# Dilated attention in an encoder trunk: the products of probabilities and values of two heads in one matmul, by halves of the residues

## The chip, the cores and the metric

The kernel runs on one core of a Trainium2 chip. Times are microseconds of device time of that core (us). The core has TensorE (PE: matmuls, with its weight loads, PEld), VectorE (DVE), ScalarE (ACT), GpSimd (POOL) and SyncE (SP, which here issues most of the transfers). Each of them works through its own queue in order and waits for the others by semaphores.

## The reference, cut to what matters

A trunk of two layers is applied to two sequences of 512 tokens. Each layer has four attention branches fed from one input projection; their gated outputs are merged and projected. The change is in the fourth branch, dilated attention: three groups of keys, each seen through its own stride and window, with one softmax over all of them in the end.

```
D_GROUPS = ((128, 1), (512, 4), (2048, 16))
...
o, lse = _banded_attention(to_strided(q), to_strided(k), to_strided(v), window // (2 * dil), D_BLOCK, HEAD_DIM ** -0.5)
...
w = softmax(stack(lses, axis=0), axis=0)
o = einsum('nbthg,nbthgd->bthgd', w, stack(outs, axis=0))
```

The branch has four query heads and two key and value heads, so that two query heads share a key and a value head. That is the pair that the kernel works on.

## The kernel before, in words

A pass is one layer of one sequence; there are four: layer 0 of the first and the second sequence, then layer 1 of both. In a pass everything lies with the channel on the partitions and the 512 tokens along the free axis. Tokens are ordered by their residue modulo 4: four blocks of 128 columns, one for each residue.

Precision comes from splitting. A float32 value is rounded to the matmul's type (hi) and the difference kept (lo), so that a projection takes three matmuls (`mm3`, L153 to L155: hi by hi, hi by lo, lo by hi), and a product with the softmax's probabilities takes two, one with the high part of the probabilities and one with the low part. The weights of the value matrix hold hi in 64 columns and lo in the other 64, so the output has 128 rows, and `finish` (L326) adds the upper 64 to the lower: a copy on ScalarE (L330), a sum on VectorE (L331). `split` (L169) is a cast on ScalarE (L170) and a subtraction on VectorE (L171).

`dilated_pair` (L463) works on one pair of heads. Scores of all groups are computed by matmuls into two PSUM banks named ss (L479, L383, L384), and moved with scale and mask to a score buffer s of 128 x 2048 for each head (L481, L492): columns 0 to 511 for the group of stride 4, 512 to 1023 for stride 16, 1024 to 2047 for the near group in four parts n. Then, head by head: the maximum over the keys (a fold on VectorE, an all-reduce over partitions on GpSimd, L318), its subtraction (L507, L509, L511), the exponentials (L508, L512), and the sums (L499 to L502, later L323). Last, again head by head, the products with the values go into the one PSUM bank named so: for the two strided groups 4 residues x hi and lo, each 128 columns (L522, L523); for the near group 4 parts x hi and lo, each 256 columns (L527, L532). `finish` empties the bank before the next head may use it.

The same bank so and the same two buffers s serve the heads of the other three branches (`dense_head`, L353, and `window_pair`, L403), the loading of the inputs (`load`, `begin`) and so on. Before, s is a tag with two buffers: whoever takes one waits until every reader of the tile that lay there is done.

What stands in which order on each queue is not written by hand. The program is traced step by step (the table `steps`, L800: both pairs of the fourth branch first, D of 1 and D of 0, then the latents LAT, part of the gates G, the latent heads A, and so on), and a scheduler then moves each instruction ahead to where its model of the engines has a free place, by the instruction's place in the trace. So matmuls of later projections fill TensorE while a softmax is under way. Weights come through SP's queue into three buffers wr (L125), are rounded on ScalarE (L131) into wh, and their low parts either computed on VectorE (L110) or, where an earlier pass has stored them, loaded (L134). GpSimd's queue holds the all-reduces alone.

Of the kernel before, what the change touches and what calls it, by code (L numbers as in the profile page):

```python
# [13 lines left out]
P = 128  # L14
T = 512
# [13 lines left out]
def trunk(ctx, tc, x0, x1, wp, wr, wu, wg, wb, wm, wo, vec, rope, msk, eye, y0, y1):  # L29
# [18 lines left out]
    for args in first:  # L48
        new(*args)

# [10 lines left out]
    def pso():  # L61
        return bank("so", 1)
# [4 lines left out]
    def f(ap):  # L67
        return ap.bitcast(F32)
# [257 lines left out]
    def finish(y, rows, o):  # L326

        a, b = rows
        u = new("u", [P, T], F32, 2)
        nc.scalar.copy(out=u[a:b], in_=o[64:128])  # L330
        tt(out=y[a:b], in0=o[0:64], in1=u[a:b], op=ALU.add)  # L331
# [21 lines left out]
    def dense_head(scores, v, scale):  # L353

        s = new("s", [P, 4 * T], F32, 2)
# [47 lines left out]
    def window_pair(q, k, v, z, l, sink):  # L403
        ss = [new("s", [P, 4 * T], F32, 2) for _ in range(2)]
# [58 lines left out]
    def dilated_pair(qs, ks_, vs, z, l):  # L463

        ss = [new("s", [P, 4 * T], F32, 2) for _ in range(2)]
# [28 lines left out]
        for h in range(2):  # L494
# [18 lines left out]
            tots.append(fold(ALU.add))  # L513
        y = new("yf", [P, T], F32, 1)
        for h in range(2):
            s = ss[h]
            o = pso()
            for gi in (1, 2):
                ph, pl = halves(s[:, (gi - 1) * 512 : gi * 512])
                for c in range(4):  # L520
                    sl = slice(c * P, (c + 1) * P)
                    mm(o[:, sl], vs[gi][:, c, :], ph[:, sl], start=gi + c == 1, stop=False, skip_group_check=True)  # L522
                    mm(o[:, sl], vs[gi][:, c, :], pl[:, sl], start=False, stop=False, skip_group_check=True)  # L523
            ph, pl = halves(s[:, 1024:1536])
            for n in (0, 1):
                for x in (ph, pl):
                    mm(span(o, *D_Q[n]), vs[0][:, D_K[n], :], span(x, *D_Q[n]), start=False, stop=False, skip_group_check=True)  # L527
            ph, pl = halves(s[:, 1536:2048])
            for n in (2, 3):
                for x in (ph, pl):  # L530
                    w = by4(x[:, (n - 2) * 256 : (n - 1) * 256])
                    mm(span(o, *D_Q[n]), vs[0][:, D_K[n], :], w, start=False, stop=n == 3 and x is pl, skip_group_check=True)  # L532
            finish(y, (64 * h, 64 * h + 64), o)
            rr.append(total(tots[h]))
# [5 lines left out]
    def load(l, q_, xin, yout):  # L540
        src = xin if l == 0 else saved[q_]
        xt = []
        for h in range(2):
            xl = new("s", [P, 4 * T], F32, 2)
# [23 lines left out]
    def begin(xin):  # L568
# [5 lines left out]
        early = [new("s", [P, 4 * T], F32, 2) for _ in range(2)]  # L574
# [448 lines left out]
```

## Time and profile before

| what | value |
|---|---|
| median of 3 runs | 2161.22 us (2159.58 to 2166.14) |
| the profiled execution | 2158.01 us, its span 2156.2 us |
| instructions | 29144, of them 9550 matmuls |
| granted TensorE clock, mean | 0.989 |
| GpSimd | 419.3 us busy, 19% |
| moved by DMA | 402.29 MB |

The span is the time from the first to the last instruction of the one profiled execution. An engine's busy time is the sum of its instructions' durations without overlap; a matmul's duration holds its way through the array, and matmuls overlap, so that what a matmul costs in a row of them is read from the distance between starts. The chain of waits is followed back from the last instruction: at each step to what released it, or to the instruction before it on its engine. A row of a group of instructions gives line, engine, operation, output and inputs, shape and count, and behind the bar the busy time and the mean in ns, then the idle time before them and who ended it. Lines are those of the kernel before; the lines of the changed kernel are higher by up to 28 behind the products, and by 8 ahead of it.

### The profile page before, as it was taken

How to read it: one execution, taken by the hardware profiler on the slowest of the kernel's cores; microseconds unless marked ns; L12 is line 12 of the kernel's file. 1: busy time of each engine (PE TensorE's matmuls, PEld its weight loads, DVE VectorE, ACT ScalarE, POOL GpSimd, SP SyncE). 2: the span in 40 equal slices, each digit the busy share in tenths (PEclk: the TensorE clock that was granted, in tenths of full speed). 3: DMA queues.
4: the chain of work that ended last, by engine and by line, in shares of the span. 5: the costliest groups of instructions: out<-in, count | busy, mean ns of one | idle time of the engine just before them, and what ended most of it. 6: DMA issues, size and time to landing. Idle time of an engine off the chain costs nothing.

```text
span 2156.2 us, 29144 instructions
## 1 busy us (share of the span) xinstructions
PE 2089.8 (97%) x9550; PEld 1714.5 (80%) x9550; DVE 1795.5 (83%) x3113; ACT 1310.9 (61%) x2229; POOL 419.3 (19%) x145
## 2 busy tenths in 40 slices
PE   7999989999999999999999999999999999999998
PEld 5887778877887787887888877888878887788887
DVE  7999999987489998997537999898866889997725
ACT  6746765544576777755456576754556757685434
POOL 0032213320002230222001322132200232122200
PEclk9999999999999999999999999999999999999999
DMA  6443444556877566678675434545666544455565
GB/s 216 162 148 116 152 140 154 183 186 207 284 247 226 177 227 220 222 243 280 216 232 164 150 120 142 164 155 181 224 203 226 156 152 133 149 161 166 182 215 182
DMA packets 207656, 402.29 MB, mean 187 GB/s; under 512 B 23312, under 2 KB 32016, under 8 KB 206736
## 3 DMA queue, kind: packets, MB, share of 16 engines
q1 hardware_dynamic: 199008, 383.62, 54.7%
q10 hardware_dynamic: 8496, 16.81, 2.3%
q8 instruction: 75, 1.23, 0.2%
q14 instruction: 77, 0.63, 0.1%
HBM read 306.49 MB, written 93.85 MB: 186 GB/s over the span
## 4 chain that ended last, share of the span: by engine, by line
PE 75%; DVE 14%; DMA 4%; ACT 3%; issue 2%; SPq 0%; POOL 0%; DVEq 0%; ACTq 0%; POOLq 0%
PE mm L153 22%; PE mm L154 22%; PE mm L155 22%; DMA wr<-wp 2%; DVE wl L110 2%; DVE ph L171 1%; PE so L375 1%; PE so L374 1%; DMA s<-x 1%; PE ss L383 1%; PE ss L384 1%; ACT wh L131 1%; PE mi L300 1%; ACT rs L242 1%; PE ss L154 1%
## 5 line engine op out<-in xcount | busy, mean ns | idle before, releaser
L153 PE MATMUL mm<-xn,wh 128*128 128x512 f32 x1992 | 782.3, 393 | 3.8 <-ACT wh L131 2.0
L154 PE MATMUL mm<-xn,wh 128*128 128x512 f32 x1992 | 780.1, 392 | 5.1 <-DVE xn L556 5.1
L155 PE MATMUL mm<-xn,wl 128*128 128x512 f32 x1992 | 780.1, 392 | 1.0 <-DMA wl<-lo 1.0
L131 ACT CAST wh<-wr 128x512 fp32r<-128x512 f32 (+1 forms) x596 | 385.7, 651 | 344.5 <-PE mm L154 228.1
L153 PEld LDWEIGHTS mm<-xn,wh 128*128 128x128 f32 x1992 | 374.8, 188 | 83.2 <-ACT wh L131 3.2
L154 PEld LDWEIGHTS mm<-xn,wh 128*128 128x128 f32 x1992 | 375.0, 188 | 81.2 <-DVE xn L556 5.4
L155 PEld LDWEIGHTS mm<-xn,wl 128*128 128x128 f32 x1992 | 374.9, 188 | 80.0 <-DMA wl<-lo 2.3
L323 POOL PARTITION_ALL_REDUCE mr<-mr x64 | 247.9, 3873 | 521.1 <-DVE mr L379 252.6
L318 POOL PARTITION_ALL_REDUCE mr<-mr x64 | 129.2, 2019 | 924.8 <-DVE mr L502 533.0
L110 DVE TENSOR_TENSOR wl<-wr,wh 128x512 fp32r<-128x512 f32 (+2 forms) x304 | 238.6, 786 | 37.5 <-ACT wh L131 20.9
L171 DVE TENSOR_TENSOR ph<-s,ph 128x512 fp32r<-128x512 f32 (+2 forms) x256 | 186.6, 735 | 15.8 <-ACT ph L170 11.9
L170 ACT CAST ph<-s 128x512 fp32r<-128x512 f32 (+2 forms) x256 | 145.0, 577 | 23.3 <-PE so L451 8.2
L242 ACT COPY rs<-mm 32x512 f32<-32x512 f32 x240 | 138.7, 578 | 25.7 <-DVE rx L237 20.3
L153 PE MATMUL mm<-qk,wh 128*128 128x512 f32 (+1 forms) x328 | 124.2, 383 | 8.3 <-ACT wh L131 5.8
L154 PE MATMUL mm<-qk,wh 128*128 128x512 f32 (+1 forms) x328 | 124.8, 382 | 5.8 <-DVE qk L835 5.6
L155 PE MATMUL mm<-qk,wl 128*128 128x512 f32 (+1 forms) x328 | 124.5, 381 | 0.6 <-DVE wl L110 0.3
L153 PE MATMUL mm<-y,wh 128*128 128x512 f32 x256 | 102.8, 405 | 14.0 <-DVE mg L768 11.6
L746 DVE SCALAR_TENSOR_TENSOR th<-th,mm 128x512 f32<-128x512 f32 x96 | 65.2, 681 | 59.0 <-PE mm L155 56.2
L745 ACT ACTIVATE th<-mm 128x512 f32<-128x512 f32 x96 | 57.3, 597 | 81.6 <-PE mm L155 80.9
L155 PE MATMUL mm<-y,wl 128*128 128x512 f32 x256 | 101.2, 395 | 0.0
L154 PE MATMUL mm<-y,wh 128*128 128x512 f32 x256 | 101.1, 395 | 0.0
L359 ACT ACTIVATE s<-ss 128x512 f32<-128x512 f32 x128 | 71.3, 596 | 34.2 <-DVE ph L171 17.3
(183 smaller groups left out, 3292.6 us busy)
## 6 DMA issues: line engine op xcount, KB each, us to landing
wr<-wp SPq DMA_DIRECT2D x310, 256.0 KB, 2.9
wl<-lo SPq DMA_DIRECT2D x250, 256.0 KB, 2.9
wr<-wm SPq DMA_DIRECT2D x192, 320.0 KB, 3.2
lo<-wl SPq DMA_DIRECT2D x200, 256.0 KB, 2.0
lo<-wl SPq DMA_DIRECT2D x96, 320.0 KB, 2.3
wl<-lo SPq DMA_DIRECT2D x96, 320.0 KB, 3.1
wr<-wo SPq DMA_DIRECT2D x68, 256.0 KB, 3.5
wr<-wg SPq DMA_DIRECT2D x64, 256.0 KB, 2.8
```

Of the source, the lines that this page charges most:

```text
L110: tt(out=lo[:, :n], in0=raw[:, :n], in1=f(hi[:, :n]), op=ALU.subtract)
L131: nc.scalar.copy(out=hi[:, :n], in_=raw[:, :n])
L153: mm(ps, wh, xh, start=first, stop=False)
L154: mm(ps, wh, xl, start=False, stop=False)
L155: mm(ps, wl, xh, start=False, stop=last)
L170: ins = nc.scalar.copy(out=hi, in_=src)
L171: tt(out=lo, in0=src, in1=f(hi), op=ALU.subtract)
L242: nc.scalar.copy(out=xs[c : c + 32], in_=ps[o : o + 32])
L318: nc.gpsimd.partition_all_reduce(m, t, P, RED.max)
L323: nc.gpsimd.partition_all_reduce(s, t, P, RED.add)
L359: act(out=s[:, j * T : (j + 1) * T], in_=ps, func=AF.Copy, scale=scale)
L746: stt(out=th, in0=th, scalar=1.0, in1=pb, op0=ALU.add, op1=ALU.mult)
```

## The change

The two score buffers become the two halves of one tile `both_s`, taken in turn by `scores_tile`; `dilated_pair` begins with half 0, so that its two heads lie in one tile at a fixed distance. The products then take columns of both heads at once. The 512 columns of the bank so are 2 heads x 256; the pass over the four residues is cut into two halves of two residues each, and `finish` takes a range of columns. The sums, maxima and exponentials are as they were.

```diff
+    both_s = new("s", [P, 2, 4 * T])
+    turn = [0]
+
+    def scores_tile():
+
+        turn[0] ^= 1
+        return both_s[:, turn[0] ^ 1, :]
...
-    def finish(y, rows, o):
+    def finish(y, rows, o, t=slice(0, T)):
...
-        nc.scalar.copy(out=u[a:b], in_=o[64:128])
-        tt(out=y[a:b], in0=o[0:64], in1=u[a:b], op=ALU.add)
+        nc.scalar.copy(out=u[a:b, t], in_=o[64:128])
+        tt(out=y[a:b, t], in0=o[0:64], in1=u[a:b, t], op=ALU.add)
...
-        ss = [new("s", [P, 4 * T], F32, 2) for _ in range(2)]
+        turn[0] = 0
+        ss = [scores_tile() for _ in range(2)]
...
+        def both(f):
+            hi = new("ph", [P, T], F32R, 6)
+            lo = new("ph", [P, T], F32R, 6)
+            src = f(both_s)
+            hh, ll = (x.rearrange("p (h x) -> p h x", h=2) for x in (hi, lo))
+            if len(src.shape) == 4:
+                hh, ll = (x.rearrange("p h (n x) -> p h n x", n=2) for x in (hh, ll))
+            split(hh, ll, src)
+            return hi, lo
+
+        for half in range(2):
+            o = pso()
+            o4 = o.rearrange("p (h c i) -> p h c i", h=2, c=2)
+            for gi in (1, 2):
+                base = (gi - 1) * 512 + 256 * half
+                pair = both(lambda s: s[:, :, base : base + 256])
+                for c in range(2):
+                    for x in pair:
+                        x4 = x.rearrange("p (h c i) -> p h c i", h=2, c=2)
+                        mm(o4[:, :, c, :], vs[gi][:, 2 * half + c, :], x4[:, :, c, :], start=gi + c == 1 and x is pair[0], stop=False, skip_group_check=True)
+            pair = both(lambda s: s[:, :, 1024 + 256 * half : 1280 + 256 * half])
+            for n in (0, 1):
+                a, b = D_Q[n][0] // 4, D_Q[n][1] // 4
+                for x in pair:
+                    x4 = x.rearrange("p (h c i) -> p h c i", h=2, c=2)
+                    mm(o4[:, :, :, a:b], vs[0][:, D_K[n], :], x4[:, :, :, a:b], start=False, stop=False, skip_group_check=True)
...
+            t = slice(256 * half, 256 * half + 256)
+            for h in range(2):
+                finish(y, (64 * h, 64 * h + 64), o[:, 256 * h : 256 * h + 256], t)
         for h in range(2):
-            s = ss[h]
-            o = pso()
-            for gi in (1, 2):
-                ph, pl = halves(s[:, (gi - 1) * 512 : gi * 512])
-                for c in range(4):
-                    sl = slice(c * P, (c + 1) * P)
-                    mm(o[:, sl], vs[gi][:, c, :], ph[:, sl], start=gi + c == 1, stop=False, skip_group_check=True)
-                    mm(o[:, sl], vs[gi][:, c, :], pl[:, sl], start=False, stop=False, skip_group_check=True)
...
-            finish(y, (64 * h, 64 * h + 64), o)
             rr.append(total(tots[h]))
```

In the changed kernel the products stand in L545 (strided groups), L551 and L557 (near group), `split` in L178 and L179, `finish` in L338 and L339, the eviction of scores in L490 and L501 (L367 in `dense_head`), the exponentials in L517 and L521, a projection's three matmuls in L161 to L163. The scheduler makes of it another order. TensorE before, the first pair of the first pass, first head (`so` is the result's bank, `ph` the split probabilities, `v` the values, `mm` a projection that fills):

```order
L523 MATMUL so_699<-ph_701,v_561 128x128
L522 MATMUL so_699<-ph_700,v_561 128x128
L523 MATMUL so_699<-ph_701,v_561 128x128
L522 MATMUL so_699<-ph_700,v_561 128x128
L523 MATMUL so_699<-ph_701,v_561 128x128
L522 MATMUL so_699<-ph_700,v_561 128x128
L523 MATMUL so_699<-ph_701,v_561 128x128
L522 MATMUL so_699<-ph_712,v_564 128x128
L154 MATMUL mm_1144<-xn_65_217,wh_1167 128x512
L523 MATMUL so_699<-ph_713,v_564 128x128
L522 MATMUL so_699<-ph_712,v_564 128x128
```

The same pair in the changed kernel, both heads, first half of the residues:

```order
L545 MATMUL so_696<-ph_697,v_560 128x2x128
L163 MATMUL mm_1468<-xn_61_204,wl_1472 128x512
L161 MATMUL mm_1468<-xn_62_208,wh_1491 128x512
L162 MATMUL mm_1468<-xn_62_208,wh_1491 128x512
L545 MATMUL so_696<-ph_698,v_560 128x2x128
L545 MATMUL so_696<-ph_697,v_560 128x2x128
L545 MATMUL so_696<-ph_698,v_560 128x2x128
L545 MATMUL so_696<-ph_705,v_563 128x2x128
L163 MATMUL mm_1468<-xn_62_208,wl_1492 128x512
L161 MATMUL mm_1468<-xn_63_212,wh_1491 128x512
L162 MATMUL mm_1468<-xn_63_212,wh_1491 128x512
L545 MATMUL so_696<-ph_706,v_563 128x2x128
```

Eight narrow products of a group become four wide ones for both heads, and the first product of the pair stands at row 423 of TensorE's queue where it stood at row 346: projections went ahead of it. VectorE before, the end of the first pair (`s_613` is the second head's buffer; `s_1189` belongs to the second pair, and takes the first head's buffer):

```order
L171 TENSOR_TENSOR ph_733<-s_612,ph_732 128x512
L247 TENSOR_TENSOR rx_1076<-rx_1076,rs_1077 128x512
L502 TENSOR_TENSOR mr_680<-mr_680,s_613 128x4x64
L481 SCALAR_TENSOR_TENSOR s_1189<-ss_1191,band_340 128x4x64
L481 SCALAR_TENSOR_TENSOR s_1189<-ss_1196,band_340 128x4x64
L110 TENSOR_TENSOR wl_1449<-wr_1446,wh_1448 128x512
L350 SCALAR_TENSOR_TENSOR z_1187<-th_1185,mm_1144 128x512
L272 TENSOR_TENSOR qk_1085<-rx_1076,qk_1085 64x512 x2
L110 TENSOR_TENSOR wl_1497<-wr_1494,wh_1496 128x512
L507 TENSOR_TENSOR s_613<-s_613,mr_685 128x1024
```

The same place in the changed kernel, where all score buffers are the one tile `s_79`:

```order
L179 TENSOR_TENSOR ph_753<-s_79,ph_752 128x512
L339 TENSOR_TENSOR yf_695<-so_696,u_729 64x256
L213 TENSOR_SCALAR ms_1451<-rs_1449 128x16
L118 TENSOR_TENSOR wl_1637<-wr_1634,wh_1636 128x512
L490 SCALAR_TENSOR_TENSOR s_79<-ss_1176,band_339 128x4x64 x2
L490 SCALAR_TENSOR_TENSOR s_79<-ss_1181,band_339 128x4x64 x2
L186 TENSOR_SCALAR nw_1454<-ms_1451 128x16
L339 TENSOR_TENSOR yf_695<-so_696,u_732 64x256
```

Before, the second pair's first scores are evicted (L481) ahead of the second head's exponentials (their subtraction is L507); after, they stand (L490) behind the split of the second half of the residues (`ph_753`), and the bank so is emptied in pieces of 64x256 (L339).

More of the change, by code (lines that the diff above doesn't have):

```diff
@@ L353, in dense_head @@
     def dense_head(scores, v, scale):
-        s = new("s", [P, 4 * T], F32, 2)
+        s = scores_tile()
         for j in range(4):
@@ L463, in dilated_pair @@
     def dilated_pair(qs, ks_, vs, z, l):
-        ss = [new("s", [P, 4 * T], F32, 2) for _ in range(2)]
+        turn[0] = 0
+        ss = [scores_tile() for _ in range(2)]
         def part(h, n):
@@ L514, in dilated_pair @@
         y = new("yf", [P, T], F32, 1)
-        for h in range(2):
-            s = ss[h]
-            o = pso()
-            for gi in (1, 2):
-                ph, pl = halves(s[:, (gi - 1) * 512 : gi * 512])
-                for c in range(4):
-                    sl = slice(c * P, (c + 1) * P)
[L522 to L532, printed above, removed]
-            finish(y, (64 * h, 64 * h + 64), o)
+        def both(f):
[7 more added lines that the diff above has]
+            return hi, lo
@@ new lines, in dilated_pair @@
+        for half in range(2):
[14 more added lines that the diff above has]
+                    mm(o4[:, :, :, a:b], vs[0][:, D_K[n], :], x4[:, :, :, a:b], start=False, stop=False, skip_group_check=True)
+            pair = both(lambda s: s[:, :, 1536:2048].rearrange("p h (n x) -> p h n x", n=2)[:, :, :, 128 * half : 128 * half + 128])
+            for n in (2, 3):
+                a, b = D_Q[n][0] // 4, D_Q[n][1] // 4
+                for x in pair:
+                    x5 = x.rearrange("p (h n c i) -> p h n c i", h=2, n=2, c=2)
+                    mm(o4[:, :, :, a:b], vs[0][:, D_K[n], :], x5[:, :, n - 2, :, :], start=False, stop=n == 3 and x is pair[1], skip_group_check=True)
+            t = slice(256 * half, 256 * half + 256)
+            for h in range(2):
+                finish(y, (64 * h, 64 * h + 64), o[:, 256 * h : 256 * h + 256], t)
@@ L543, in load @@
         for h in range(2):
-            xl = new("s", [P, 4 * T], F32, 2)
+            xl = scores_tile()
             nc.scalar.dma_start(out=xl.rearrange("p (k t) -> p k t", k=4), in_=src[:, 4 * h : 4 * h + 4, :])
@@ L573, in begin @@
         src = wp[0, T_D + 6 * 1]
-        early = [new("s", [P, 4 * T], F32, 2) for _ in range(2)]
+        early = [scores_tile() for _ in range(2)]
         xt = [early[k // 4][:, (k % 4) * T : (k % 4 + 1) * T] for k in range(NK)]
```

## The prediction

> **What bounds the kernel now.** I read the page first, then the chain of waits in four stretches, then the stretches' busy time, then single instructions. The page's busy lines and the chain:
>
> ```profile
> span 2156.2 us, 29144 instructions
> PE 2089.8 (97%) x9550; PEld 1714.5 (80%) x9550; DVE 1795.5 (83%) x3113; ACT 1310.9 (61%) x2229; POOL 419.3 (19%) x145
> PE 75%; DVE 14%; DMA 4%; ACT 3%; issue 2%; SPq 0%; POOL 0%; DVEq 0%; ACTq 0%; POOLq 0%
> ```
>
> TensorE looks full, but a quarter of the chain runs elsewhere, so it matters where the fourth branch lies on it. That branch comes first in each of the four passes (layer 0 prompt, layer 0 sample, layer 1 prompt, layer 1 sample), as two pairs of heads. The chain of waits, one line per pass, over the branch and the first latent heads behind it (60 to 300, 560 to 840, 1100 to 1370 and 1630 to 1890 us), as a share of each stretch:
>
> ```profile
> by line: PE mm L153 19.6%; PE mm L154 19.2%; PE mm L155 18.8%; DVE wl L110 4.0%; issue 3.8%; DVE ph L171 1.8%; PE ss L154 1.8%; PE ss L155 1.7%; PE mm L689 1.5%; PE ss L153 1.3%; DVE mg L768 1.3%; PE mi L300 1.2%; PE ss L479 1.2%; PE so L37
> ...
> by line: DMA wr<-wp 15.3%; issue 6.7%; DVE wl L110 5.8%; PE mm L153 5.8%; PE mm L154 5.6%; PE mm L155 5.4%; DVE ph L171 4.0%; ACT wh L131 3.3%; ACT rs L242 3.3%; DMA lo<-wl 2.2%; ACT wh L148 2.0%; DVE qk L171 1.4%; DMA wl<-lo 1.3%; DVE s L3
> ...
> by line: PE mm L153 18.1%; PE mm L155 17.7%; PE mm L154 17.7%; DVE ph L171 3.1%; issue 2.6%; DVE qk L171 2.1%; DVE wl L110 1.9%; DVE mr L379 1.9%; DVE s L368 1.6%; DVE rstd L179 1.4%; PE ss L479 1.4%; PE mm L689 1.3%; PE so L522 1.3%; POOL
> ...
> by line: PE mm L153 25.2%; PE mm L154 25.0%; PE mm L155 24.9%; PE ss L153 1.5%; PE mi L300 1.5%; PE ss L154 1.4%; PE ss L479 1.4%; PE ss L155 1.4%; PE mm L689 1.4%; PE so L522 1.4%; PE so L523 1.3%; PE so L375 1.1%; PE ss L384 1.1%; PE ss L
> ```
>
> In the fourth pass it is TensorE alone, the branch's own products (L522, L523) on it. In the third TensorE holds it too, L522 at 1.3% of 270 us being 3.5 us, the whole group of a pass; only later does VectorE take over. In the second pass it runs through weight transfers and their splitting, with no product of the branch among the large shares. The first pass is mixed; its pieces in order of time:
>
> ```profile
> 124.68 0.52 PE so L527 x4
> 129.43 0.35 PE so L532 x3
> 130.71 1.39 PE mm L689 x6
> 138.99 0.68 DVE yf L341
> 159.93 1.14 DVE s L507
> 177.69 1.23 DVE s L507
> 191.14 0.53 PE so L527 x4
> ```
>
> Up to about 131 us, that is through the first pair's products, it is TensorE; from 139 to 189 us mostly VectorE, preparing the second pair. So five of eight pairs have their products on TensorE's part of the chain, three lie where something else ends last. The busy time of VectorE and TensorE in these four places (columns: stretch, length, then each engine) says how near the second bound is:
>
> ```profile
> 60.00:200.00 140.00, 135.16 (x644) 110.62 (x643) 135.46 (x248) 88.73 (x152) 29.91 (x10) 0.98 0.45 144
> 600.00:740.00 140.00, 133.65 (x644) 109.40 (x644) 122.85 (x227) 95.02 (x164) 28.06 (x11) 0.99 0.69 224
> 1150.00:1270.00 120.00, 116.89 (x572) 97.05 (x571) 113.78 (x208) 75.14 (x129) 34.35 (x11) 0.99 0.44 140
> 1680.00:1790.00 110.00, 110.00 (x548) 92.00 (x547) 100.84 (x188) 70.57 (x120) 29.44 (x10) 1.00 0.51 151
> ```
>
> **The change part by part: products.** Before, each pair of heads issues 2 x 16 matmuls of 128 columns (L522, L523) and 2 x 8 of 256 (L527, L532), 8192 columns. After, 2 x 16 of 256: the same columns in 32 instructions. What one costs is its distance to the next start. TensorE in order of time, fourth pass, then the first (there 256 columns as two runs of 128, the shape the change writes):
>
> ```profile
> 1718.18 0.22 PE L522 MATMUL so<-ph,v 128*128 128x128 f32 x1
> 1718.24 0.45 PE L153 MATMUL mm<-xn,wh 128*128 128x512 f32 x1
> 1718.52 0.39 PE L154 MATMUL mm<-xn,wh 128*128 128x512 f32 x1
> 1718.75 0.40 PE L155 MATMUL mm<-xn,wl 128*128 128x512 f32 x1
> ...
> 1719.28 0.27 PE L522 MATMUL so<-ph,v 128*128 128x128 f32 x1
> ...
> 1720.84 0.69 PE L527 MATMUL so<-ph,v 128*128 128x256 f32 x4
> 1721.36 0.40 PE L154 MATMUL mm<-xn,wh 128*128 128x512 f32 x1
> ...
> 144.08 0.28 PE L384 MATMUL ss<-qk,qk 128*128 128x256 f32 x1
> 144.20 0.28 PE L383 MATMUL ss<-qk,qk 128*128 128x256 f32 x1
> 144.32 0.28 PE L384 MATMUL ss<-qk,qk 128*128 128x256 f32 x1
> ```
>
> From 1719.28 to 1720.84 fourteen narrow matmuls start: 0.111 us each. Four of 256 columns take 0.52 us (0.13 each), and 0.12 in the first pass. So 128 columns cost nearly what 256 do. Per pair 32 x 0.111 = 3.55 us become 16 x 0.12 = 1.92 (2.08 at 0.13): 1.47 to 1.63 us less; I take 1.6, since the 0.12 row has the new shape. Eight pairs: 12.8 us of TensorE time. On the chain are five: 5 x 1.6 = 8.0 us.
>
> **Evacuation.** A head's result leaves PSUM as one 512-column copy on ScalarE and one sum on VectorE; now as two of 256 each. The rows (old shape, then the nearest rows with 256 columns from PSUM):
>
> ```profile
> L331 DVE TENSOR_TENSOR yf<-so,u 64x512 f32<-64x512 f32 x64 | 43.4, 679 | 4.1 <-ACT u L330 3.2
> L860 DVE TENSOR_TENSOR mg<-mm,u 128x256 f32<-128x256 f32 x16 | 6.7, 423 | 13.6 <-PE mm L155 8.3 <-DMA u<-x 5.3
> L330 ACT COPY u<-so 64x512 f32<-64x512 f32 x64 | 37.3, 583 | 27.7 <-PE so L375 14.1 <-PE so L452 6.8 <-PE so L532 5.4
> L170 ACT CAST v<-mi 128x256 fp32r<-128x256 f32 x56 | 20.8, 372 | 13.4 <-DVE v L171 8.6 <-PE mi L300 4.4
> ```
>
> Per pair VectorE pays 4 x 0.423 - 2 x 0.679 = 0.33 us more, ScalarE 4 x 0.372 - 2 x 0.583 = 0.32. ScalarE is 61% busy and not on the chain there: nothing, and at worst the same 0.32 in the three pairs off TensorE. VectorE's counts in those three: 1.0 us. Without cover it is 2.6 us for all eight.
>
> **Splitting and buffers.** The probabilities are still split by 64 casts and 64 subtractions of 128x512, only of two heads' halves; runs in place of one block cost nothing in the nearest row (L511, which reads one operand in four runs of 64: 417 ns, against L860's 423). What moves is when. The first head's products no longer start before the second head's exponentials, and both score buffers stay taken until the second half has been split. VectorE around this place in the first pass:
>
> ```profile
> L511 DVE TENSOR_TENSOR s<-s,mr 128x256 f32<-128x256 f32 x32 | 12.0, 417 | 0.0
> ...
> 118.36 1.06 ACT L512 ACTIVATE s<-s 128x1024 f32<-128x1024 f32 x1 [0.21 <-DVE s L511]
> ...
> 120.71 0.67 DVE L171 TENSOR_TENSOR ph<-s,ph 128x512 fp32r<-128x512 f32 x1
> ...
> 126.32 0.67 DVE L171 TENSOR_TENSOR ph<-s,ph 128x512 fp32r<-128x512 f32 x1
> ...
> 127.25 0.73 DVE L481 SCALAR_TENSOR_TENSOR s<-ss,band 128x256 f32<-128x256 f32 x2
> ```
>
> Behind the last exponential (119.4 us) four splits come, the last done at 127.0; now eight must, 4 x 0.67 = 2.7 us more of VectorE at the least. Queued behind them are the next pair's score evictions (L481) and behind these its scores on TensorE, which holds two score banks only. I cost this delay at nothing: later projections fill TensorE there (the order puts more of them ahead of the late products), and the evictions catch up before the latent heads. Uncovered it is 2.7 to 7.6 us a pair (the second end is all the time from 119.4 to 127.0 once more), and below nothing it cannot be, since nothing is released earlier.
>
> **Sum.** -8.0 + 1.0 = -7.0 us. The profiled execution took 2158.0 us (span 2156.2), so 2151.0; the median of the runs shown is 2161.2, which gives 2154.2.
>
> **Rivals.** (1) *TensorE's saving stays whole*: the other three pairs gain too, because TensorE is 95 to 97% busy there and the chain's other members have little slack. -12.8 + 1.0 = -11.8: 2149.4. Against it speaks the second pass's chain of transfers, which a faster product doesn't shorten.
>
> (2) *VectorE takes it all*: where it is 97% busy (135.46 of 140 us), TensorE arrives earlier at a wait that ends no earlier, and in the later passes too behind the branch. Then only the evacuation is left: +2.6, so 2163.8.
>
> (3) *Narrow matmuls were not dear*: the lone L522 at 1718.18 is followed after 0.06 us. If that were the price, 32 x 0.06 = 1.92 equals the new 1.92, and the time is +1.0 to +2.6, about 2163. Against it: the L153 behind it is followed after 0.28 us, where the next L154 is after 0.23, so the rest is paid there; and the run of fourteen at 0.111. The Trainium skill, TensorE: Matmul & The Clock Gate, section "Wait — 56ns, not 53.3ns?", has the spacing of warm matmuls as columns over 2.4 GHz plus about 2.5 ns, 56 ns at 128; by that rule the change saves TensorE nothing. The run of fourteen disagrees with it at 111 ns.
>
> (4) *Slower: the late release of the score buffers binds.* In the three pairs whose chain leads over VectorE or transfers, each delay of 2.7 to 7.6 us (5 in the middle) goes into the chain: 3 x 5 - 7.0 = +8.0, so 2169.2. It decides from 7.0 / 3 = 2.3 us a pair. For it: VectorE has no slack there and runs its queue in order, with weight splits behind. Against it: TensorE's waits for the eviction of scores are small, and few:
>
> ```profile
> PE ss L153 <- ACT s L359: 2.0, 1, 2.0
> ```
>
> **How the numbers follow.** Forecast 0.42, (1) 0.22, (2) 0.15, (3) 0.05, (4) 0.16. About 0.3%, 6.5 us, is what a measurement of this kernel can tell from no change. The forecast lies just beyond it, so its chance is divided, 0.28 beyond and 0.14 within; with (1) faster is 0.50, same 0.34 with (2) and (3), slower 0.16. The range begins below (1), at 2144: 1.63 instead of 1.6 a pair, no new evacuation on the chain, and the spread of the runs (2159.58 below the median by 1.6) are worth 3 us, the rest is left to the new order. It ends at 2168, just short of (4)'s middle.
>
> **What would show it.** Right: L545, L551 and L557 at about 0.12 us apart; TensorE's products 1.6 us a pair shorter; third and fourth pass some 3 us shorter each, the second unchanged; VectorE's busy time up by about 2.6 us. Wrong: spacing of 0.2 us or more for two runs of 128; new TensorE waits of over 2 us behind score evictions (L367, L490, L501) in the first two passes, which is (4); or passes three and four no shorter, which is (2).

## The result, and the profile after

The changed kernel takes 2175.48 us, median of 6 runs (2172.41 to 2177.53), beside 2158.85 us for the kernel before, median of 6 (2152.50 to 2166.14). The ratio is 1.0070, with a 95% interval of 1.0056 to 1.0084: slower by about 15 us by the ratio (the medians lie 16.6 us apart). That is outside the range of the prediction, on the side of its fourth rival and beyond that rival's 2169.2.

The page's busy lines and the chain of the changed kernel's profiled execution (2172.76 us, mean granted clock 0.981 where the kernel before had 0.989):

```profile
span 2171.0 us, 28989 instructions
PE 2089.9 (96%) x9422; PEld 1710.0 (79%) x9422; DVE 1799.0 (83%) x3129; ACT 1316.4 (61%) x2245; POOL 404.2 (19%) x145
PE 79%; DVE 15%; issue 2%; ACT 2%; DMA 2%; POOL 0%; SPq 0%; DVEq 0%; ACTq 0%; POOLq 0%
```

128 matmuls are gone, and TensorE's busy time is what it was: 2089.9 us, 2089.8 before. By the prediction's price for the removed work (12.8 us) it should have been 2077.0, so 12.9 us of other matmuls became slower. The idle rest of the span, span minus busy, went from 66.4 to 81.1 us. So: -12.8 for the products, +12.9 for slower matmuls, +14.7 for idle time, +14.8 together, which is the difference of the spans. The slower matmuls are those at half clock: a mean of 0.981 over 2171 us is 2 x 0.019 x 2171 = 82 us at half clock, and 0.989 over 2156 was 47. This takes the clock as either full or half; rows further down bear that out, with matmuls 0.43 us apart instead of 0.23.

The products' groups and the evacuation's, changed kernel:

```profile
L545 PE MATMUL so<-ph,v 128*128 128x256 f32 x128 | 21.9, 296 | 8.7 <-ACT ph L178 4.4 <-DVE ph L179 4.2
L557 PE MATMUL so<-ph,v 128*128 128x256 f32 x64 | 13.3, 300 | 0.0
L551 PE MATMUL so<-ph,v 128*128 128x256 f32 x64 | 12.4, 306 | 1.6 <-DVE ph L179 1.6
L339 DVE TENSOR_TENSOR yf<-so,u 64x256 f32<-64x256 f32 x32 | 13.2, 413 | 5.4 <-ACT u L338 4.9
L338 ACT COPY u<-so 64x256 f32<-64x256 f32 x32 | 11.8, 368 | 19.0 <-DVE yf L339 16.7 <-PE so L557 1.9
```

The strided products (L545) are half as many, and they now wait 8.7 us; before, L522 and L523 waited 0.9 us in all for the splits. The evacuation's rows, 413 and 368 ns, are close to the estimates of the prediction (423 and 372). VectorE's busy time rose by 3.5 us, where 2.6 had been reckoned.

**Where the time went.** Most of the loss lies in one place of each pass: from the products of the branch's second pair to the scores of the first latent heads. TensorE's busy time and granted clock there, first in the kernel before (columns: stretch, length, then each engine, and the clock behind POOL):

```profile
150.00:200.00 50.00, 46.41 (x213) 36.68 (x212) 49.27 (x92) 31.16 (x53) 11.01 (x4) 0.93 0.43 135
715.00:745.00 30.00, 27.00 (x126) 21.19 (x125) 29.60 (x47) 20.93 (x37) 5.79 (x2) 0.94 0.52 166
1240.00:1280.00 40.00, 36.89 (x170) 28.96 (x168) 39.43 (x63) 26.44 (x45) 6.92 (x3) 0.96 0.39 119
1770.00:1800.00 30.00, 30.00 (x147) 23.83 (x145) 28.70 (x44) 20.48 (x35) 4.32 (x2) 1.00 0.47 146
```

The same place in the changed kernel, whose later passes reach it some 10 to 15 us later:

```profile
150.00:200.00 50.00, 41.34 (x165) 31.30 (x164) 49.11 (x86) 24.82 (x40) 10.32 (x4) 0.86 0.39 124
725.00:755.00 30.00, 25.90 (x107) 19.89 (x106) 29.71 (x49) 23.38 (x40) 5.43 (x1) 0.83 0.52 165
1250.00:1290.00 40.00, 34.53 (x145) 26.76 (x144) 38.65 (x59) 27.28 (x47) 10.60 (x4) 0.83 0.34 105
1785.00:1815.00 30.00, 25.70 (x114) 20.73 (x113) 25.88 (x42) 21.26 (x37) 2.15 (x1) 0.89 0.32 102
```

Idle, length minus busy, was 3.6 + 3.0 + 3.1 + 0 = 9.7 us and is 8.7 + 4.1 + 5.5 + 4.3 = 22.5. At half clock, twice the missing part of the clock times the length, were 14 us and are 44. These 150 us hold 12.8 of the 14.7 us of new idle time, and 30 of the 35 us more at half clock. The fourth pass is the plainest, because it was full and at full clock before. TensorE there, changed kernel, in order of time (start, duration, what; the wait in brackets):

```profile
1780.78 0.64 PE L545 MATMUL so<-ph,v 128*128 128x256 f32 x4
...
1782.76 0.40 PE L161 MATMUL mm<-qk,wh 128*128 128x512 f32 x1
...
1785.43 0.52 PE L545 MATMUL so<-ph,v 128*128 128x256 f32 x3
...
1786.92 0.77 PE L557 MATMUL so<-ph,v 128*128 128x256 f32 x4
1791.58 0.79 PE L161 MATMUL ss<-qk,qk 96*128 96x512 f32 x1 [3.89 <-ACT s L367]
1792.17 0.63 PE L162 MATMUL ss<-qk,qk 96*128 96x512 f32 x1
1792.60 0.63 PE L163 MATMUL ss<-qk,qk 96*128 96x512 f32 x1
1793.03 0.63 PE L161 MATMUL ss<-qk,qk 96*128 96x512 f32 x1
...
1794.31 0.63 PE L161 MATMUL mm<-qk,wh 128*128 128x512 f32 x1
```

TensorE has nothing to do for 3.89 us, until ScalarE has evicted a score bank of the first latent head (L367); then its matmuls start 0.43 us apart instead of 0.23. What ScalarE did meanwhile:

```profile
1785.87 0.62 ACT L178 CAST ph<-s 128x512 fp32r<-128x512 f32 x1 [1.82 <-PE so L545]
1786.51 0.62 ACT L342 COPY mr<-mr 64x512 f32<-64x512 f32 x1
1787.15 0.62 ACT L178 CAST ph<-s 128x512 fp32r<-128x512 f32 x1
...
1790.29 0.62 ACT L178 CAST ph<-s 128x512 fp32r<-128x512 f32 x1
1790.93 1.08 ACT L367 ACTIVATE s<-ss 128x512 f32<-128x512 f32 x2
```

The eviction stands in ScalarE's queue behind three casts of the late splits (L178); between these lie casts and copies for other work. The first of the three waited 1.82 us for TensorE to release a buffer of the split. The products that read that buffer (L545) came as late as 1785.43: until then matmuls of projections, from 1782.76 on, ran ahead of them in TensorE's queue. ScalarE then works without a pause, and the eviction starts at 1790.93. For TensorE these scores are next in its queue, and it takes them in order: more projections stand behind the scores, the first at 1794.31. Whether any of them could have run during the wait is not shown. The granted clock of the wait and of the 5 us behind it:

```profile
1787.00:1792.00 5.00, 1.11 (x6) 0.83 (x5) 4.94 (x11) 4.88 (x9) 0.00 (x0) 0.77 0.00 0
1792.00:1797.00 5.00, 5.00 (x14) 3.85 (x14) 4.89 (x9) 1.60 (x4) 0.00 (x0) 0.54 0.05 13
```

In the second row TensorE is busy all 5 us at 0.54 of its clock: the wait is paid a second time. The other passes have pieces at half clock in this place too, with waits that end behind other instructions. Three groups of TensorE's waits, changed kernel (in total, times, the longest):

```profile
PE ss L161 <- ACT s L367: 4.9, 2, 3.9
PE so L545 <- ACT ph L178: 4.4, 2, 3.3
PE so L545 <- DVE ph L179: 4.2, 4, 2.7
```

The 3.3 us lie in the first pass, the 2.7 in the third; in the second pass no wait of the stretch is over 1.2 us. These groups are not the largest of the whole execution. That one, 16.3 us in 13 waits behind VectorE's L796, had its like before (11.6 us in ten, there L768).

### The profile page after: what moved, and what is told of

The parts are those of the page before. It is cut to its first block, busy times and chain, and to the rows that moved or that the text cites. A ratio compares the mean times of both kernels' runs of the same rounds, so it can differ in the third digit from the quotient of the medians.

```text
span 2171.0 us, 28989 instructions
## 1 busy us (share of the span) xinstructions
PE 2089.9 (96%) x9422; PEld 1710.0 (79%) x9422; DVE 1799.0 (83%) x3129; ACT 1316.4 (61%) x2245; POOL 404.2 (19%) x145
## 4 chain that ended last, share of the span: by engine, by line
PE 79%; DVE 15%; issue 2%; ACT 2%; DMA 2%; POOL 0%; SPq 0%; DVEq 0%; ACTq 0%; POOLq 0%
PE mm L161 23%; PE mm L162 23%; PE mm L163 23%; DVE wl L118 2%; DVE ph L179 1%; DVE s L376 1%; PE so L383 1%; PE so L382 1%; PE ss L392 1%; PE ss L391 1%; DMA wr<-wp 1%; DVE mr L369 1%; PE mi L308 1%; PE ss L161 1%; PE ss L488 1%
## 5 line engine op out<-in xcount | busy, mean ns | idle before, releaser
L161 PE MATMUL mm<-xn,wh 128*128 128x512 f32 x1992 | 783.7, 393 | 5.3 <-ACT xn L583 2.1
L163 PE MATMUL mm<-xn,wl 128*128 128x512 f32 x1992 | 780.4, 392 | 1.2 <-DMA wl<-lo 1.2
L161 PEld LDWEIGHTS mm<-xn,wh 128*128 128x128 f32 x1992 | 376.0, 189 | 85.9 <-ACT xn L583 2.5
L163 PEld LDWEIGHTS mm<-xn,wl 128*128 128x128 f32 x1992 | 375.8, 189 | 80.0 <-DMA wl<-lo 2.4
L331 POOL PARTITION_ALL_REDUCE mr<-mr x64 | 232.1, 3627 | 503.6 <-DVE mr L387 223.3
L326 POOL PARTITION_ALL_REDUCE mr<-mr x64 | 129.8, 2028 | 945.8 <-DVE mr L511 526.2
L179 DVE TENSOR_TENSOR ph<-s,ph 128x512 fp32r<-128x512 f32 (+2 forms) x256 | 195.4, 771 | 5.5 <-ACT ph L178 4.1
L178 ACT CAST ph<-s 128x512 fp32r<-128x512 f32 (+2 forms) x256 | 144.1, 578 | 28.0 <-PE so L459 9.8
L250 ACT COPY rs<-mm 32x512 f32<-32x512 f32 x240 | 138.6, 578 | 27.5 <-DVE rx L245 21.6
L161 PE MATMUL mm<-qk,wh 128*128 128x512 f32 (+1 forms) x328 | 124.6, 385 | 10.7 <-ACT wh L139 5.7
L161 PE MATMUL mm<-y,wh 128*128 128x512 f32 x256 | 106.0, 417 | 20.1 <-DVE mg L796 15.1
L163 PE MATMUL mm<-qk,wl 128*128 128x512 f32 (+1 forms) x328 | 123.9, 381 | 0.3 <-DVE wl L118 0.3
L163 PE MATMUL mm<-y,wl 128*128 128x512 f32 x256 | 103.2, 403 | 0.0
L162 PE MATMUL mm<-y,wh 128*128 128x512 f32 x256 | 103.1, 403 | 0.0
L367 ACT ACTIVATE s<-ss 128x512 f32<-128x512 f32 x128 | 74.9, 597 | 30.1 <-DVE ph L179 12.0
```

The source lines that it names most:

```text
L161: mm(ps, wh, xh, start=first, stop=False)
L162: mm(ps, wh, xl, start=False, stop=False)
L163: mm(ps, wl, xh, start=False, stop=last)
L178: ins = nc.scalar.copy(out=hi, in_=src)
L179: tt(out=lo, in0=src, in1=f(hi), op=ALU.subtract)
L250: nc.scalar.copy(out=xs[c : c + 32], in_=ps[o : o + 32])
```

## The experiments

Theory A: the delay that the prediction cost at nothing is the loss; the first head's products now start late, and the buffers come free late. Theory B: the evacuation in four pieces. Theory C: the wider products save less than reckoned, or nothing. Theory D: the change merely moves the scheduler's order. Ratios are against the kernel before on the same chip, with 95% intervals.

**The buffers alone.** The kernel before, with the two score buffers as halves of one tile and its own products:

```diff
+    both_s = new("s", [P, 2, 4 * T])
...
-        ss = [new("s", [P, 4 * T], F32, 2) for _ in range(2)]
+        turn[0] = 0
+        ss = [scores_tile() for _ in range(2)]
```

> The change's buffer part alone: the score buffers are halves of one tile, taken in turn, with the products of the kernel before, head by head. Theory (tied heads: the products of a pair begin only after both heads' exponentials and hold both score buffers until the last split; this, not the tile, makes TensorE wait): within 6 us of the kernel before, since each head's half is still released by itself. Rival (one tile): the scheduler's dependencies on one tile are the cost, then 10 to 25 us slower. Rival (scatter): any change of the traced program sends the scheduler another way by some 10 us in either direction, then this differs from the kernel before by 5 to 15 us without a reason of its own.

2159.48 us, ratio 0.9987 (0.9976 to 0.9999). One tile in place of two buffers costs nothing. The four stretches:

```profile
150.00:200.00 50.00, 44.25 (x197) 33.69 (x196) 49.08 (x89) 28.21 (x48) 10.70 (x4) 0.91 0.40 128
715.00:745.00 30.00, 27.56 (x126) 21.46 (x126) 29.64 (x48) 22.48 (x38) 4.28 (x2) 0.94 0.71 225
1240.00:1280.00 40.00, 35.27 (x162) 27.06 (x161) 39.05 (x60) 25.03 (x41) 10.32 (x3) 0.96 0.42 135
1770.00:1800.00 30.00, 30.00 (x149) 24.38 (x148) 29.49 (x47) 21.45 (x38) 5.45 (x2) 1.00 0.52 161
```

Idle 12.9 us and 16 us at half clock, near the kernel before, and the fourth pass is still full.

**The late start alone.** To that, one VectorE instruction that reads a column of each quarter of the second head's exponentials, times zero, into the first head's. The first head's products so wait for the second head's exponentials. No other instruction is changed; but the first head's splits come later with its products, so its buffer and its result are released later too:

```diff
+        e0, e1 = (s.rearrange("p (c t) -> p c t", c=4)[:, :, 0:1] for s in ss)
+        stt(out=e0, in0=e1, scalar=0.0, in1=e0, op0=ALU.mult, op1=ALU.add)
         for h in range(2):
```

> The kernel halves_only (score buffers as halves of one tile, which took 2159.5 us, narrow products head by head) with one small instruction of VectorE in each pair that writes four columns of the first head's probabilities back unchanged but reads the second head's: no product of the first head begins before the second head's exponentials. Buffers are released piece by piece, as in the change. Theory (late start): 10 to 20 us slower than halves_only, with waits and half clock where the second pair meets the first latent head. Rival (evacuation in halves, which took 13.7 us by itself): within 5 us of halves_only. Rival (scatter of the order): anything within 10 us of halves_only, with the loss at places that have nothing to do with the pair.

2174.58 us, ratio 1.0061 (1.0043 to 1.0078), 15.1 us over the kernel with the joined buffers alone. The stretches:

```profile
150.00:200.00 50.00, 42.01 (x182) 32.78 (x182) 48.55 (x86) 26.32 (x43) 10.60 (x4) 0.90 0.36 120
715.00:745.00 30.00, 24.94 (x114) 19.10 (x113) 29.55 (x46) 21.48 (x37) 6.24 (x3) 0.94 0.49 159
1240.00:1280.00 40.00, 37.18 (x162) 28.82 (x161) 38.71 (x63) 24.76 (x41) 11.40 (x4) 0.87 0.35 113
1785.00:1815.00 30.00, 26.21 (x127) 21.62 (x127) 28.89 (x44) 22.05 (x37) 5.87 (x2) 0.89 0.33 105
```

Idle 19.7 us, at half clock 31. The fourth pass shows a loss like that of the changed kernel, 3.8 us idle and a clock of 0.89, without its products or its evacuation. Its longest wait there, 2.02 us, ends behind VectorE (L720), not behind an eviction of scores. Theory A has its first half, together with the later release that a late start brings with it.

**The late release alone, and both.** In the kernel before, a tiny sum reads the first head's buffer beside the second head's last split, so that the whole buffer is held until then; and this together with the tie above:

```diff
+            if h == 1:
+                held = new("ms", [P, 16], F32, 2)
+                tt(out=held[:, 0:1], in0=ss[0][:, 0:1], in1=f(pl[:, 0:1]), op=ALU.add)
             finish(y, (64 * h, 64 * h + 64), o)
```

> The kernel before with one small instruction of VectorE a pair that reads the first head's buffer after the second head's last split: the products start as early as before, but the first head's buffer is released as late as the second's, as a whole. If the release as a whole is what cost tied_heads its 95 us: 60 to 95 us slower than the kernel before. If its late start did: within 10 us of the kernel before.

> The kernel before, with its narrow products and its own buffers, and two small instructions of VectorE in each pair: one writes four columns of the first head's probabilities back unchanged but reads the second head's, so that no product of the first head begins before the second head's exponentials; one reads the first head's buffer after the second head's last split, so that it is released no earlier. Theory (tied heads): 15 to 27 us slower than the kernel before, the loss of the change without its saving of 12 us, with TensorE waits of over 2 us and the half clock at the second pair of each pass. Rival (one tile, or the quartered evacuation): within 5 us of the kernel before.

2198.66 us (1.0174, 1.0144 to 1.0205) and 2256.90 us (1.0440, 1.0419 to 1.0462). Both are far dearer than the change, and both lie outside what was expected: 37 us where 60 to 95 or less than 10 had been named, 95 where 15 to 27 had. The added read holds the whole buffer, while the change frees it in pieces as they are split. So the 37 us of the first show which way a late release goes and are an upper end for it, not its price in the change.

**The products narrow again.** The changed kernel with its strided products issued head by head, 128 columns each, in the same place:

```diff
-                        mm(o4[:, :, c, :], vs[gi][:, 2 * half + c, :], x4[:, :, c, :], ...)
+                        for h in range(2):
+                            mm(o4[:, h, c, :], vs[gi][:, 2 * half + c, :], x4[:, h, c, :], ...)
```

> The changed kernel with each product of a strided group issued by head again, 128 columns instead of 256: 16 matmuls more a pair, 0.111 instead of 0.06 us for 128 columns, so 12 to 13 us more of TensorE work in all; splits, buffers and evacuation as in the change. If TensorE's saving is real and only covered by new waits elsewhere: 8 to 16 us slower than the changed kernel. If the saving falls into waits anyway (TensorE arrives early at a wait that does not move): within 4 us of the changed kernel.

2188.87 us, ratio 1.0124 (1.0101 to 1.0146): 13.4 us over the changed kernel. The pieces of the chain in the fourth pass show the price of one, first here (sixteen in 1.74 us, 0.109 each):

```profile
1744.92 1.51 PE so L546 x14
1760.22 1.74 PE so L546 x16
```

then in the changed kernel, 256 columns in two runs (four in 0.47 us, 0.12 each):

```profile
1780.94 0.47 PE so L545 x4
```

The saving of TensorE's time is real by these rows, and theory C falls. The same edit on the fastest kernel, which a later part makes:

> The kernel paired_near_first (2153.9 us) with the products of the strided groups issued by head, 128 columns instead of 256. If its gain is the wide products' saving: 9 to 16 us slower than paired_near_first. If only its order is lucky: within 5 us of it.

2168.47 us, ratio 1.0038 (1.0023 to 1.0053), 14.6 us over that kernel. In ratios the two steps are 0.0054 and 0.0071, that is 12 and 15 us, each uncertain by some 5 from the spread of the runs.

**The evacuation.** Three edits: the kernel before with `finish` in two ranges of 256 columns; the same with 384 and 128; and the changed kernel with one copy of 64 x 512 on ScalarE for a half, in place of two of 64 x 256.

```diff
-            finish(y, (64 * h, 64 * h + 64), o)
+            for c in (0, 256):
+                a, b = 64 * h, 64 * h + 64
+                t = slice(c, c + 256)
+                u = new("u", [P, T], F32, 2)
+                nc.scalar.copy(out=u[a:b, t], in_=o[64:128, t])
+                tt(out=y[a:b, t], in0=o[0:64, t], in1=u[a:b, t], op=ALU.add)
```

> The kernel before with the evacuation of each head's product in two ranges of 256 columns, as the change has it, and nothing else. Theory (tied heads): 0 to 3 us slower, the 2.6 us of VectorE work at most. Rival (evacuation): the longer hold of the result's bank makes the products of the next head late, 8 us or more. Rival (scatter): 5 to 15 us in either direction.

> The kernel finish_halves (2175.4 us: the kernel before with two ranges of 256 columns in the evacuation) with ranges of 384 and 128 columns instead: the same instructions, the same column sum, durations that differ by some 0.1 us. Rival (evacuation): 2175, since as many instructions hold the bank as long. Rival (scatter): elsewhere by 5 us or more, as the scheduler's order comes out another way.

> The changed kernel with the two copies of ScalarE (64x256) of each half made one of 64x512; VectorE's four sums a pair stay. Theory (late start): within 5 us of the changed kernel, since the products begin as late as before. Rival (evacuation): 5 to 13 us faster than the changed kernel, as the bank is free earlier. Rival (scatter): 5 to 15 us in either direction.

2175.36 us (1.0059, 1.0042 to 1.0076), 2178.47 us (1.0069, 1.0046 to 1.0092) and 2177.07 us (1.0071, 1.0056 to 1.0086). The first two read like a verdict for theory B. The third doesn't bear it out: fewer, longer copies give nothing back. The instructions added come to no more than some 3 us on either engine; 14 to 16 us from them is an effect on the order, or a cause that wasn't found.

**How far the order alone goes.** The kernel before with the near group's products written ahead of the strided groups'. No instruction is added or taken away:

```diff
+            ph, pl = halves(s[:, 1024:1536])
...
             for gi in (1, 2):
                 ph, pl = halves(s[:, (gi - 1) * 512 : gi * 512])
...
-            ph, pl = halves(s[:, 1024:1536])
```

> The kernel before with the products of the near group traced ahead of those of the strided groups: the same instructions, another order. A measure of scatter. If the order's scatter is small: within 4 us of the kernel before. If it is as large as the differences in question: 5 to 15 us in either direction.

2169.58 us, ratio 1.0040 (1.0025 to 1.0055). The same in the changed kernel:

> The changed kernel with the near group's products ahead of the strided groups' in each half: the columns that the second pair of heads writes first come free two splits sooner, those that a latent head writes first two splits later. Release binds: 5 us or more in one direction, with the waits moved from one kind of place to the other (second pair, first latent head). Start binds: within 5 us of the changed kernel, the fourth pass's half clock as it was.

2184.30 us, ratio 1.0110 (1.0082 to 1.0138). By what was expected, a difference of over 5 us in the changed kernel spoke for the late release; but the same edit costs as much in the kernel before, where the heads are not joined, so it can't be told from the order. So a change of order alone is worth 8 to 9 us here. Theory D is no theory of this change, but it limits what a difference of 10 us between two of these kernels can prove.

**Giving the buffers back sooner.** The changed kernel with a second bank for the second half, taken from the four of the projections, and the groups in the outer loop, so that both halves of a group are split together:

```diff
-        for half in range(2):
-            o = pso()
-            for gi in (1, 2):
+        banks = [pso(), pmm()]
+        for gi in (1, 2):
+            for half in range(2):
```

> The changed kernel with a second bank (one of the four of the projections) for the second half of the residues, and the two halves split and multiplied group by group: the score columns that the next heads write first come free after two splits instead of five, while the start stays as late. Theory in its first form (late release binds): 5 to 15 us faster than the changed kernel. Theory (late start binds): within 5 us. Against both: the projections lose a bank for a while, which would show as TensorE waits for ScalarE or VectorE in them.

2317.91 us, ratio 1.0724 (1.0708 to 1.0740). TensorE's longest waits in this kernel:

```profile
PE so L545 <- ACT ph L178: 130.5, 8, 16.9
PE so L545 <- DVE ph L179: 17.6, 8, 2.2
```

130.5 us in eight waits, one of about 16 us a pair, before its first products. That is nearly the whole 142 us over the changed kernel. The projections, which fill TensorE while a softmax runs, have one bank less; that they stop for this is argued from the place of the wait, not tried apart. With the softmax side by side, as in the next part:

> Both of these edits together. If start and release both cost: faster than either, below the kernel before (2150 to 2158 us). If only one binds: as the better of the two within 4 us.

2282.63 us, ratio 1.0557 (1.0541 to 1.0572). Both runs lie far outside every range that was named for them, so neither tells what an earlier release is worth.

**Both heads' softmax side by side.** If the late start is the loss, the second head's exponentials should come sooner. The maxima of both heads are written first, then subtraction and exponentials, then both sums:

```diff
-            m = top(fold(ALU.max))
+        tops = [top(fold(h, ALU.max)) for h in range(2)]
+        for h in range(2):
+            s, m = ss[h], tops[h]
...
-            tots.append(fold(ALU.add))
+        tots += [fold(h, ALU.add) for h in range(2)]
```

> The changed kernel with the two heads' softmax traced side by side: both maxima, then both subtractions and exponentials, then both sums, so that the second head's exponentials come sooner behind the first head's. The same instructions. Theory (late start and what follows from it: waits at the second pair and the first latent head, and half clock there): 5 to 15 us faster than the changed kernel, with less half clock between the pair's scores and the branch's projection. Rival (evacuation in halves, or scatter alone): no tendency, within 8 us of the changed kernel either way, and the half clock there as it was.

> The kernel before (narrow products, head by head) with the softmax of the two heads traced side by side. The first head's products begin later than before, the second's sooner. Theory (late start): 0 to 10 us slower than the kernel before. If side by side is a better order by itself: 5 us or more faster, and then a gain of the kernel paired says nothing on the start.

In the changed kernel 2169.03 us, ratio 1.0027 (1.0010 to 1.0044); in the kernel before 2177.87 us, ratio 1.0068 (1.0051 to 1.0084). It helps the kernel that needs both heads at once, by 0.0043 or 9 us, and hurts the one that could start with a single head, by 15. That is theory A's prediction in sign; the 15 us are more than the 0 to 10 that it had named, and the 9 us are no more than the order alone has moved. The profiled execution of the first, 2160.62 us, is the fastest of its ten, so its stretches are not set beside the others. With the near group first as well:

> The kernel paired (2169.0 us) with the near group's products first. Release binds: 5 us or more from paired in either direction. Start binds: within 5 us of paired, below the changed kernel.

2153.91 us (2151.08 to 2158.73, 10 runs), ratio 0.9967 (0.9953 to 0.9981): faster than both kernels. The stretches:

```profile
150.00:200.00 50.00, 41.22 (x170) 32.75 (x169) 49.43 (x86) 27.07 (x47) 10.79 (x4) 0.87 0.39 126
715.00:745.00 30.00, 29.05 (x143) 22.86 (x143) 29.57 (x51) 23.61 (x44) 4.76 (x3) 1.00 0.70 237
1240.00:1280.00 40.00, 35.71 (x168) 27.33 (x168) 39.14 (x63) 27.18 (x48) 10.19 (x3) 1.00 0.42 134
1770.00:1800.00 30.00, 30.00 (x145) 23.62 (x144) 29.10 (x47) 22.12 (x39) 2.08 (x1) 1.00 0.44 137
```

Idle 14.0 us, at half clock 13: in these stretches the passes two to four are at full clock, and the fourth is full. Its two parts don't add up, though: near group first cost 9 us in the changed kernel by itself and saved 15 behind the paired softmax. That this order is good is measured; why that one is, is not. The 15 us are also outside the 5 us that had been named for a late start as the only cause. Last, the two paired kernels with the single copy of the evacuation:

> The kernel paired with one copy of ScalarE for each half instead of two. Evacuation binds: 5 us or more faster than paired, below the kernel before. Start binds: within 5 us of paired, and below the changed kernel.

> The kernel paired_near_first with one copy of ScalarE for each half instead of two. Evacuation binds: 3 us or more faster. Otherwise within 5 us of it; if more than 5 us slower, the scheduler's order alone moves the time by that much.

2168.36 us (1.0034, 1.0020 to 1.0048), no different from the paired kernel, and 2164.54 us (1.0013, 1.0003 to 1.0022), 10.6 us worse than the best. So the evacuation's form can't be judged by this edit: it does nothing, nothing and harm in three kernels.

The five kernels whose stretches are shown, side by side:

| kernel | TensorE idle in the four stretches | at half clock | ratio |
|---|---|---|---|
| before | 9.7 us | 14 us | 1 |
| joined buffers | 12.9 | 16 | 0.9987 |
| joined buffers, late start | 19.7 | 31 | 1.0061 |
| changed | 22.5 | 44 | 1.0070 |
| changed, paired, near group first | 14.0 | 13 | 0.9967 |

Half of the time at half clock is lost, if TensorE is busy in it. From the second row to the third that makes at most 6.8 + 7.5 = 14.3 us, against 15.1 measured; from the fourth to the fifth 8.5 + 15.5 = 24.0 at most, against 21.6.

**The fourth pass tells order from late start.** Kernels without the join that are slower by their order or their evacuation don't lose their time there. The 150 us around this place, in the changed kernel, the one with the late start alone, the kernel before with `finish` in two ranges, and the kernel before with the softmax side by side:

```profile
1700.00:1850.00 150.00, 145.71 (x669) 119.36 (x668) 134.28 (x240) 100.64 (x171) 38.88 (x14) 0.98 0.46 141
1700.00:1850.00 150.00, 146.21 (x692) 121.07 (x691) 133.31 (x235) 98.99 (x165) 39.60 (x15) 0.98 0.45 140
1700.00:1850.00 150.00, 149.43 (x722) 123.55 (x721) 138.34 (x248) 102.72 (x177) 40.68 (x14) 1.00 0.46 145
1700.00:1850.00 150.00, 150.00 (x725) 124.36 (x725) 140.96 (x244) 101.42 (x172) 43.99 (x15) 1.00 0.48 146
```

The last two are 13 and 15 us slower than the kernel before (by the ratios), yet TensorE is idle here for 0.6 us in the one and not at all in the other, at full clock. In the kernel before with the near group first it isn't idle here either. In the first two it is idle for 4.3 and 3.8 us, at a mean clock of 0.98. So in this pass those edits of order and evacuation make no such loss by themselves, and the late start makes it by itself. Two things stay open even here. The kernel with the late release alone is idle for 7.8 us, so a late release can do the same, and how much of it is in the change is not known. And the changed kernel with the single copy is idle for 1.8 us, so the evacuation may add to the loss. In the other passes nothing separates the causes so plainly.

## Why the prediction was wrong

**Products: right, and in one point perhaps too careful.** 32 matmuls of about 0.11 us became 16 of 0.12. Rival (3) is refuted. With it goes, for these matmuls in a row, the rule of 56 ns at 128 columns in the Trainium skill, TensorE: Matmul & The Clock Gate, section "Wait — 56ns, not 53.3ns?": the runs show 109. That only five of eight pairs would gain was not borne out: undoing the edit costs 13.4 and 14.6 us, nearer to all eight (12.8) than to five (8.0), and the second of them excludes 8.0 by its interval. That interval doesn't cover the 8 to 9 us that the order alone can move, so this speaks against five pairs and doesn't settle it. The chain of one execution names what ended last; it did not tell what a shorter TensorE is worth there.

**Evacuation: right in its rows,** 413 and 368 ns. Its effect on the time stays open: finishing in two ranges made the kernel before 14 us slower, and undoing part of it in the changed kernel gave nothing.

**The step that failed** is this one: "I cost this delay at nothing: later projections fill TensorE there (the order puts more of them ahead of the late products), and the evictions catch up before the latent heads." The projections fill TensorE only as far as they stand ahead of what it will wait for; those ahead of the late products made these later still, and those behind the scores wait with them. The evictions don't catch up: L367 in the fourth pass stands behind the late casts, and TensorE waits 3.89 us. The late start, with the later release that it brings, costs 15.1 us. It is not a shift of work by a few us with cover; in the changed kernel TensorE is idle for longer, by 1.1 to 5.1 us, at the end of the branch in every pass.

**The sum had no term for the clock.** Even the range for "uncovered", 2.7 to 7.6 us a pair, counted waiting only. Around the waits of this place TensorE ran at half clock for 7 to 14 us in each pass, and about half of the loss is there: 12.9 us of slower matmuls beside 14.7 of idle time. The trace of before had the evidence, a clock of 0.93 to 0.96 in the very stretches where TensorE waited.

**Rival (4)** had the direction, and its sign in the trace appeared, a wait of over 2 us behind L367. But it appeared in the fourth pass, which it had left out: it counted three pairs, all in the first two passes, and all four passes lose. In the first two no wait behind an eviction of scores is over 1.0 us. And what held the eviction last in the fourth pass is ScalarE's queue, where no pause stands ahead of it, rather than a score buffer that was still taken. The fourth was held safe because TensorE alone was on its chain. That says that nothing else had been late, not how late the others could come before they would be. Its chance of 0.16 was too low for a delay whose cover rested on an argument from the order.

**What stays open.** Joined buffers, late start and wider products would give about 0.9987 + 0.0074 - 0.0059 = 1.0002 by their measured steps and the 12.8 us; the changed kernel is at 1.0070. So the late start has a measured step for about half of the 28 us that lie between the saving and the result (15 of slowdown and 12.8 of saving). Its place in the fourth pass ties that step to the change; how much of it in the other passes is order is not known. Some 15 us more belong to the later release, the evacuation, or the order into which all this falls. No edit here separates them, as edits that only move the order cost 8 to 9 us by themselves.

## What to carry to other kernels

A join that lets one instruction serve two producers makes both wait for the later one: price the wait of the consumer's engine at the end of the stage, not only the instructions saved, and see whether the producers can be brought side by side first. That an engine is 100% busy in a stretch doesn't say how late the others may come; ask which of its filling work stands ahead of the instruction that will wait, and which behind it. Where a few us of waiting cost as much again in clock, count each new wait of TensorE about twice.

## What the runs showed of the hardware

**Half clock behind short waits.** In the fourth pass of the changed kernel a wait of 3.89 us was followed by 5 us at a granted clock of 0.54. In the third the longest wait is 2.7 us, and the clock is 0.57, 0.50 and 0.57 in the three pieces of 5 us from 1260 us on. In the second no wait of the stretch is over 1.2 us, and the clock is 0.50 from 735 to 745 us. The Trainium skill, TensorE: Matmul & The Clock Gate, section "Part 1: The HAM clock gate", has the clock go to half after an idle window of about 3.4 us, and back after a busy one. The return in the fourth pass, after some 5 us of work, is in line with it; that the clock falls only after so long an idle time is not, by the second and the third pass.

**VectorE beside an all-reduce.** The subtraction of a split, 128 x 512, took three times as long while GpSimd's all-reduce ran. VectorE in the fourth pass of the changed kernel, then GpSimd:

```profile
1782.25 2.02 DVE L179 TENSOR_TENSOR ph<-s,ph 128x512 fp32r<-128x512 f32 x1
...
1787.76 0.69 DVE L179 TENSOR_TENSOR ph<-s,ph 128x512 fp32r<-128x512 f32 x1
```

```profile
1781.49 3.23 POOL L331 PARTITION_ALL_REDUCE mr<-mr  x1 [8.64 <-DVE mr L511]
```

The first, at 1782.25, lies inside the all-reduce and takes 2.02 us; the later one takes 0.69. The Trainium skill, SBUF — State Buffer, section "Who interferes with whom", says that a VectorE instruction with two SBUF inputs contends with a GpSimd instruction that reads SBUF; the row agrees. It is a delay of 1.3 us in one of the late splits, for each of which the prediction took 0.67.
